# Output projection of a decoder block: half of its inner dimension as seven products of halves instead of eight, with some low parts made by GpSimd

## The chip, the cores and the metric

One core of one Trainium2 chip. The metric is the device time of one execution in microseconds (us); the kernel before takes 858.08 us, the median of three runs.

## The reference, cut to what matters

The kernel computes a hybrid decoder block in float32 on 512 tokens of width 1024: a stick-breaking attention branch and an RWKV-7 branch, merged by sigmoid gates, an output projection, a squared-ReLU MLP, per-layer embeddings and a final norm. The change lies between the merge and the MLP:

```
m = sb_up * sigmoid(gate_sb) + (rw @ w_up_rw) * sigmoid(gate_rw)   # 512 x 1024, the merged tiles
x = x + m @ w_out                                                   # 1024 x 1024, the output projection
h = rms_norm(x, mlp_norm_g)                                         # input of the MLP's first product
```

## The kernel before, in words

**Products.** TensorE multiplies float32 as three products of a reduced format (fp32r): every operand is held as a high part, which ScalarE makes by a cast, and a low part, the source minus the high part, which VectorE makes by a subtraction (`split`, L266; for weights `fetch_to`, L221 and L222). Each product of a 128 x 128 block with a 128 x 512 block is then three matmuls into one PSUM tile: high by high, high by low, low by high (`mm3`, lines L237 to L239, weights stationary; `rows3`, lines L252 to L254, activations stationary and weights moving).

**Weights.** They come in units of 128 x 1024 (512 KB), in the fixed list `seq`. SyncE loads each into one of four `w_raw` buffers; `fetch_to` then casts and subtracts up to three units ahead of the one in use (`AHEAD`), as the matmuls count down in `step`. A unit named in `homes` gets buffers of its own (`wo..`), which stay until the last token tile.

**The merge.** For m = 0 to 7 (the loop at L1128) 12 matmuls multiply the RWKV branch `orw` by half a unit of `w_up_rw` into one PSUM tile; the gate `gb` (loaded by SyncE at L1132) gets a sigmoid on ScalarE (L1134); VectorE multiplies it with the PSUM tile (L1142) and adds the other branch `ga` (loaded at L1131, added at L1143); and `split` writes the high and low parts of the merged tile into `mg0` and `mg1`, 128 channels by 512 tokens each. After the last sigmoid ScalarE loads the table of logarithm and exponential (L1137). The four tiles of the residual `xs` (512 KB each) and `praw` (512 KB) are loaded ahead of the loop (L1123, L1125).

**The output projection.** A unit of `w_out` holds 256 of the 1024 inner channels for one half of the 1024 columns: units 0 to 3 are the first half of the columns, 4 to 7 the second. `by_token` (L1077) makes the first half of the columns, 4 units x 4 token tiles x 6 matmuls, into four PSUM tiles; then, for each token tile in turn, 4 units x 6 matmuls make the second half. That is 192 matmuls of 128 x 512. `taken` (L1151) adds a finished PSUM tile to `xs` and sums its squares, `scaled` (L1162) makes the row scale and writes `xsc`, and `gained` (L1083) transposes `xsc` on TensorE (L1093) and splits it into `hx0` and `hx1`, the input of the MLP (ScalarE at L1097, VectorE at L1098).

**Order.** Each engine and each DMA queue does its instructions in the order in which the program lists them; a framework works this order out from the code's order, the buffers and the dependences. GpSimd does nothing in this stretch before.

Of the kernel before, what the change touches and what calls it, by code (L numbers as in the profile page):

```python
# [10 lines left out]
F32 = mybir.dt.float32  # L11
# [7 lines left out]
P = 128  # L19
# [72 lines left out]
def tile_block(ctx: ExitStack, tc: tile.TileContext, xT, xt, pT, wts, lora, cols_d, gfin_d, consts_d, out, dbg=None):  # L92
# [5 lines left out]
    def r32(ap):  # L98
        return ap.bitcast(F32)
# [106 lines left out]
    def fetch_to(n, ahead=0):  # L206
        while state["i"] < min(n, len(seq)):
            i = state["i"]
            state["i"] += 1
            load_to(i + 1 + ahead)  # L210
            raw = made(i)
            if seq[i] in homes:
                hi, lo = homes[seq[i]]()
            elif seq[i][0] == U_S4:
                hi = wpool.tile([P, 512], F32R, name="w_hi4", bufs=1)
                lo = wpool.tile([P, 512], F32R, name="w_lo4", bufs=1)
            else:
                hi = wpool.tile([P, 1024], F32R, name="w_hi")
                lo = wpool.tile([P, 1024], F32R, name="w_lo")
            with tc.issue_after(state["hx"]) if seq[i] == (U_FF1, 4) else nullcontext():  # L220
                state["cast"] = act.copy(out=hi, in_=raw).ins  # L221
            state["wlo"] = dve.tensor_tensor(out=lo, in0=raw, in1=r32(hi), op=ALU.subtract).ins  # L222
            ready.setdefault(seq[i], []).append((hi, lo))

    def weights(*u):
# [21 lines left out]
    def rows3(ps, w, rhs, tt, k, first, last, cs=slice(0, 512)):  # L247

        xh, xl = (r[:, :, tt * P:(tt + 1) * P] for r in rhs)
        for j in range(2):  # L250
            wh, wl = (p_.rearrange("p (j f) -> p j f", j=2)[:, j, cs] for p_ in w)
            pe.matmul(ps, xh[:, k + j], wh, start=first and j == 0, stop=False, skip_group_check=True)  # L252
            pe.matmul(ps, xh[:, k + j], wl, start=False, stop=False, skip_group_check=True)  # L253
            pe.matmul(ps, xl[:, k + j], wh, start=False, stop=last and j == 1, skip_group_check=True)  # L254
            step()

    def product(ps, w, rhs, nk=KT, base=0, t=slice(0, T)):
# [5 lines left out]
            mm3(ps, w, 0, rhs, k, k == 0, k == KT - 1)  # L263
            yield

    def split(hi, lo, src):  # L266
        act.copy(out=hi, in_=src)
        state["lo"] = dve.tensor_tensor(out=lo, in0=src, in1=r32(hi), op=ALU.subtract).ins

    def sum_squares(pool_, src, k, ssum):  # L270

# [51 lines left out]
    with ExitStack() as sA:  # L323
# [43 lines left out]
        with ExitStack() as s1:  # L367
# [709 lines left out]
    def by_token(u, i, rhs, half):  # L1077
# [5 lines left out]
                rows3(pss[tt], w, rhs, tt, kk * 2, kk == 0, kk == 3)  # L1083
        return pss

    def gained(gname, half, src):

        for kp in range(KT // 2):
            ps = ps_main().rearrange("p (j t) -> p j t", j=2)
            for j in range(2):  # L1090
                for t in range(2):
                    k = kp * 2 + j
                    pe.transpose(out=ps[:, j, t * P:(t + 1) * P], in_=src[:, half * 2 + t, k * P:(k + 1) * P], identity=ident)  # L1093
# [25 lines left out]
    with ExitStack() as s3:  # L1119
        p3 = s3.enter_context(tc.tile_pool(name="p3", bufs=1))  # L1120
        mg = [pa.tile([P, KT, T], F32R, name="mg0", tag="h_lo"), p3.tile([P, KT, T], F32R, name="mg1")]
        for tt in range(TT):
            sync.dma_start(out=xs[:, tt, :], in_=xt[:, tt, :])  # L1123
        praw = p3.tile([P, 2, T], F32, name="praw")
        sync.dma_start(out=praw, in_=pT)  # L1125
        for m in range(8):

            early = {0: ("mix", "mix"), 1: ("mix", "mix"), 2: ("gg", "gg")}.get(m)  # L1128
            ga, gb = (pa.tile([P, T], F32, name=n, tag=early[j], bufs=4 if early[j] == "mix" else 2) if early else
                      p3.tile([P, T], F32, name=n, bufs=3) for j, n in enumerate(("ga", "gb")))  # L1130
            sync.dma_start(out=ga, in_=upsb[:, m, :])  # L1131
            sync.dma_start(out=gb, in_=gates[:, KT + m, :])  # L1132
            with tc.issue_after(state["norm"].ins):
                last = act.activation(out=gb, in_=gb, func=AF.Sigmoid)  # L1134
            if m == 7:
                with tc.issue_after(last.ins):
                    state["load"] = act.preload_act_table_set(LNEXP)  # L1137
            if m % 2 == 0:
                w = weights(U_UPRW, m // 2)
            ps = ps_main()  # L1140
            product(ps, w, orw, nk=4, base=m % 2 * 512)
            dve.tensor_tensor(out=gb, in0=ps, in1=gb, op=ALU.mult)  # L1142
            dve.tensor_tensor(out=ga, in0=ga, in1=gb, op=ALU.add)  # L1143
# [18 lines left out]
        def scaled(tt):  # L1162
# [8 lines left out]
        pss = by_token(U_OUT, 0, mg, 0)  # L1171
        for tt in range(TT):
            taken(pss[tt], tt, 0)
        ws = [weights(U_OUT, 4 + kk) for kk in range(4)]

        for tt in range(TT):
# [424 lines left out]
```

## Time and profile before

| what | value |
|---|---|
| times of the three runs | 859.78, 858.08, 857.35 us |
| median | 858.08 us |
| the profiled execution's own time | 858.42 us |
| its span in the trace | 856.7 us |
| granted TensorE clock, mean | 0.998 |
| busy share PE / DVE / ACT / POOL | 98% / 82% / 59% / 12% |
| the merge on TensorE | 404.3 to 425.9 us |
| the output projection on TensorE | 425.9 to 471.2 us |

Times inside the trace are us from the start of the span. PE is TensorE's matmuls, DVE is VectorE, ACT is ScalarE, POOL is GpSimd, SP is SyncE; L12 is line 12 of the kernel the row belongs to. A row's `out<-in` names the tiles; the numbers behind x are counts. Matmuls overlap each other, so the duration of one record is longer than its share of the engine.

### The profile page before, as it was taken

How to read it: one execution, taken by the hardware profiler on the slowest of the kernel's cores; microseconds unless marked ns; L12 is line 12 of the kernel's file. 1: busy time of each engine (PE TensorE's matmuls, PEld its weight loads, DVE VectorE, ACT ScalarE, POOL GpSimd, SP SyncE). 2: the span in 40 equal slices, each digit the busy share in tenths (PEclk: the TensorE clock that was granted, in tenths of full speed). 3: DMA queues.
4: the chain of work that ended last, by engine and by line, in shares of the span. 5: the costliest groups of instructions: out<-in, count | busy, mean ns of one | idle time of the engine just before them, and what ended most of it. 6: DMA issues, size and time to landing. Idle time of an engine off the chain costs nothing.

```text
span 856.7 us, 14612 instructions
## 1 busy us (share of the span) xinstructions
PE 841.8 (98%) x5606; PEld 699.0 (82%) x5606; DVE 702.6 (82%) x1247; ACT 506.8 (59%) x793; POOL 102.3 (12%) x170
## 2 busy tenths in 40 slices
PE   9999999999999999999999999999999999999996
PEld 6778788877777777777888888899889989988885
DVE  7989987896987978867773597899889988997767
ACT  7888887744436253534464675468647844783843
POOL 1332431001202111020000101000110010010000
PEclk9999999999999999999999999999999999999999
DMA  8212212231120324527960676973885489275402
GB/s 322 100 50 64 85 62 86 75 99 51 63 88 26 107 79 136 162 82 244 326 220 25 204 214 162 230 199 107 229 234 146 141 243 245 88 222 144 174 23 99
DMA packets 39333, 121.08 MB, mean 141 GB/s; under 512 B 4448, under 2 KB 4448, under 8 KB 39264
## 3 DMA queue, kind: packets, MB, share of 16 engines
q1 hardware_dynamic: 34656, 103.37, 35.5%
q0 software_dynamic: 4608, 16.78, 10.7%
q8 instruction: 44, 0.72, 0.4%
q14 instruction: 25, 0.20, 0.1%
HBM read 105.46 MB, written 10.49 MB: 135 GB/s over the span
## 4 chain that ended last, share of the span: by engine, by line
PE 87%; DVE 8%; DMA 1%; issue 1%; ACT 1%; SPq 0%; DVEq 0%; ACTq 0%
PE ps_m L237 14%; PE ps_m L238 14%; PE ps_m L239 14%; PE ps_m L252 10%; PE ps_m L253 10%; PE ps_m L254 10%; PE ps_g L863 1%; PE ps_o L543 1%; PE ps_z L551 1%; PE ps_s L991 1%; PE ps_c L982 1%; PE ps_g L953 1%; DVE LX L885 1%; DVE w_lo L222 1%; DVE own L874 1%
## 5 line engine op out<-in xcount | busy, mean ns | idle before, releaser
L221 ACT CAST w_hi<-w_raw 128x1024 fp32r<-128x1024 f32 x123 | 129.1, 1051 | 121.5 <-PE ps_m L238 71.3
L222 DVE TENSOR_TENSOR w_lo<-w_raw,w_hi 128x1024 fp32r<-128x1024 f32 x123 | 150.5, 1225 | 29.9 <-ACT w_hi L221 29.3
L237 PE MATMUL ps_m<-h_hi,w_hi 128*128 128x512 f32 x320 | 130.5, 409 | 0.1
L239 PE MATMUL ps_m<-h_hi,w_lo 128*128 128x512 f32 x320 | 128.5, 402 | 0.0
L238 PE MATMUL ps_m<-h_lo,w_hi 128*128 128x512 f32 x320 | 128.3, 401 | 0.1
L239 PEld LDWEIGHTS ps_m<-h_hi,w_lo 128*128 128x128 f32 x320 | 60.4, 189 | 11.9
L237 PEld LDWEIGHTS ps_m<-h_hi,w_hi 128*128 128x128 f32 x320 | 60.8, 190 | 10.9 <-DVE gg L724 0.4
L238 PEld LDWEIGHTS ps_m<-h_lo,w_hi 128*128 128x128 f32 x320 | 60.5, 189 | 11.2 <-DVE h_lo L400 1.3
L238 PE MATMUL ps_m<-hx,w_hi 128*128 128x256 f32 (+1 forms) x208 | 65.8, 316 | 0.0
L237 PE MATMUL ps_m<-hx,w_hi 128*128 128x256 f32 (+1 forms) x208 | 65.8, 316 | 0.0
L239 PE MATMUL ps_m<-hx,w_lo 128*128 128x256 f32 (+1 forms) x208 | 65.7, 316 | 0.0
L237 PE MATMUL ps_m<-tb,w_hi 128*128 128x256 f32 x192 | 54.3, 283 | 0.0
L238 PE MATMUL ps_m<-tb,w_hi 128*128 128x256 f32 x192 | 54.3, 283 | 0.0
L239 PE MATMUL ps_m<-tb,w_lo 128*128 128x256 f32 x192 | 54.3, 283 | 0.0
L252 PE MATMUL ps_m<-w_hi,fS 128*128 128x512 f32 x128 | 49.8, 389 | 0.0
L253 PE MATMUL ps_m<-w_lo,fS 128*128 128x512 f32 x128 | 49.8, 389 | 0.0
L254 PE MATMUL ps_m<-w_hi,fS 128*128 128x512 f32 x128 | 49.8, 389 | 0.0
L238 PEld LDWEIGHTS ps_m<-hx,w_hi 128*128 128x128 f32 x208 | 39.7, 191 | 2.9 <-DVE hx L1098 0.4
L237 PEld LDWEIGHTS ps_m<-hx,w_hi 128*128 128x128 f32 x208 | 39.7, 191 | 2.8 <-ACT hx L1097 0.2
L239 PEld LDWEIGHTS ps_m<-hx,w_lo 128*128 128x128 f32 x208 | 39.7, 191 | 2.5
L252 PE MATMUL ps_m<-w_hi,fA 128*128 128x512 f32 x96 | 37.4, 389 | 0.0
L253 PE MATMUL ps_m<-w_lo,fA 128*128 128x512 f32 x96 | 37.4, 389 | 0.0
(410 smaller groups left out, 2128.6 us busy)
## 6 DMA issues: line engine op xcount, KB each, us to landing
w_raw<-in_wts_dram SPq DMA_DIRECT2D x130, 512.0 KB, 3.7
gates<-gg SPq DMA_DIRECT2D x16, 256.0 KB, 2.0
w_raw<-in_wts_dram POOLq DMA_DIRECT2D x8, 512.0 KB, 6.7
x_in<-in_xT_dram SPq DMA_DIRECT2D x8, 256.0 KB, 5.9
tmp<-gates SPq DMA_DIRECT2D x8, 256.0 KB, 3.3
upsb<-tmp SPq DMA_DIRECT2D x8, 256.0 KB, 5.0
ga<-upsb SPq DMA_DIRECT2D x8, 256.0 KB, 5.5
gb<-gates SPq DMA_DIRECT2D x8, 256.0 KB, 5.0
```

What stands on the lines that cost most here:

```text
L221: state["cast"] = act.copy(out=hi, in_=raw).ins
L222: state["wlo"] = dve.tensor_tensor(out=lo, in0=raw, in1=r32(hi), op=ALU.subtract).ins
L237: pe.matmul(ps, wh, xh[:, k, t], start=first, stop=False, skip_group_check=skip)
L238: pe.matmul(ps, wh, xl[:, k, t], start=False, stop=False, skip_group_check=skip)
L239: pe.matmul(ps, wl, xh[:, k, t], start=False, stop=last, skip_group_check=skip)
L252: pe.matmul(ps, xh[:, k + j], wh, start=first and j == 0, stop=False, skip_group_check=True)
L253: pe.matmul(ps, xh[:, k + j], wl, start=False, stop=False, skip_group_check=True)
L254: pe.matmul(ps, xl[:, k + j], wh, start=False, stop=last and j == 1, skip_group_check=True)
L543: pe.matmul(ps_o[:, j * P:T], vv[:, j, hh, :, :].rearrange("p a d -> p (a d)"), part[:, ZB[j]:ZB[j] + ZN[j]], start=j == 2 and part is wh, ...
L551: pe.matmul(zt[b][:, :n], tri, part[:, s:s + n], start=False, stop=False, skip_group_check=True)
L863: last = pe.matmul(ps[rows, k], left[rows, k, :], rhs[rows, k], start=True, stop=True)
L874: dve.tensor_tensor(out=own8[rows], in0=own, in1=b8[rows].broadcast_to([32, 8, 32]), op=ALU.mult)
```

## The change

The first half of the inner channels (merged tiles 0 to 3, units 0, 1, 4 and 5 of `w_out`) is multiplied as a 2 x 2 product of halves with seven products and a shared set of sums (the Strassen-Winograd form) instead of eight. The halves are 256 inner channels each way, 256 tokens each way and 512 columns each way. One product of halves is 12 matmuls (`run` in `by_halves`), so the seven are 84 where eight were 96; the second half of the inner channels (units 2, 3, 6 and 7) keeps its 96, now added on top of the PSUM tiles that the seven products have left. What is new besides:

- **Sums of merged tiles** (`left_sums`): eight 128 x 256 operations on VectorE, with casts and low parts of two 128 x 1024 tiles, put into the buffers `hx0` and `hx1`.
- **Sums of weights**: T3, T2 and T1 are 128 x 1024 tiles, loaded by SyncE and added to by DMAs that GpSimd issues with accumulation; T2 is added to once more after product 2. T3 and T2 are loaded between the attention and the RWKV branch, T1 at the beginning of the merge. As operands they are called s3, s2, s4 and s6 in `seq`, and each is cast and subtracted like a unit.
- **Work between the products**: `seeded`, two copies from PSUM to PSUM on ScalarE after product 0 (product 2 goes on adding to the tiles V that were copied); `aside`, four copies from PSUM to SBUF on ScalarE; and four subtractions on VectorE with PSUM operands (`rest` and W).
- **Order on TensorE**: merged tiles 0 to 5, product 0, merged tiles 6 and 7, products 2, 1, 3, 4, 5, 6, then per token tile 12 matmuls for either half of the columns. `taken` now runs for both halves in that last loop.
- **GpSimd**: the low parts of the merged tiles 4 to 7 (128 x 512) and of units 2 and 3 (128 x 1024) go from VectorE to GpSimd.
- The loads of `xs` and `praw` are issued later, `gb` and `ga` take other buffers, tiles 0 and 1 are split for their first 256 tokens only, and the scratch of the squares has one buffer in place of two.

The diff, cut to its core:

```diff
+ORDER = (0, 2, 1, 3, 4, 5, 6)
+FROM = {0: 0, 1: 1, 5: 5}
...
-    seq += [(U_UPRW, m) for m in range(4)]
-    seq += [(U_OUT, m) for m in range(8)]
+    seq += [(U_UPRW, m) for m in range(3)] + [(U_OUT, "s", ORDER[0]), (U_UPRW, 3)]
+    seq += [(U_OUT, "s", i) for i in ORDER[1:]] + [(U_OUT, m) for m in (2, 3, 6, 7)]
...
-            state["wlo"] = dve.tensor_tensor(out=lo, in0=raw, in1=r32(hi), op=ALU.subtract).ins
+            if seq[i] in ((U_OUT, 2), (U_OUT, 3)):
+                pool.tensor_tensor(out=lo, in0=raw, in1=r32(hi), op=ALU.subtract)
+            else:
+                state["wlo"] = dve.tensor_tensor(out=lo, in0=raw, in1=r32(hi), op=ALU.subtract).ins
...
+        for t, i in ((T3, 5), (T2, 0)):
+            sync.dma_start(out=t, in_=wts[UBASE[U_OUT] + i])
+        for t, more_ in ((T3, wts[UBASE[U_OUT] + 4]), (T2, T3)):
+            pool.dma_start(out=t, in_=more_, accum_op=ALU.add)
...
+        run(0, V, True)
+        between()
+        for t2 in range(2):
+            act.copy(out=seeded[t2], in_=V[t2])
+        run(2, V, False)
+        pool.dma_start(out=T2, in_=wts[UBASE[u] + 1], accum_op=ALU.add)
+        second = aside(V)
+        run(1, seeded, False)
+        run(3, W, True)
+        run(4, V, False)
+        third = aside(W)
+        for t2 in range(2):
+            dve.tensor_tensor(out=rest[t2], in0=third[t2], in1=V[t2], op=ALU.subtract)
+        run(5, W, False)
+        for t2 in range(2):
+            dve.tensor_tensor(out=W[t2], in0=W[t2], in1=second[t2], op=ALU.subtract)
+        run(6, V, False)
+        return (seeded + V, W + rest)
...
+        sync.dma_start(out=T1, in_=wts[UBASE[U_OUT]])
+        pool.dma_start(out=T1, in_=wts[UBASE[U_OUT] + 4], accum_op=ALU.add)
...
+            n = 256 if m < 2 else T
+            split(mg[0][:, m, 0:n], mg[1][:, m, 0:n], ga[:, 0:n], dve if m < 4 else pool)
+            if m in (2, 3):
+                x, y = ups[m - 2], ga
+                left_sums(S, m - 2, y[:, 0:256], y[:, 256:T], x[:, 0:256], x[:, 256:T])
...
         for tt in range(TT):
-            ps = ps_main()
-            for kk in range(4):
-                rows3(ps, ws[kk], mg, tt, kk * 2, kk == 0, kk == 3)
-            taken(ps, tt, 1)
+            for half in range(2):
+                for kk in range(2):
+                    rows3(pss[half][tt], ws[half * 2 + kk], mg, tt, 4 + kk * 2, False, kk == 1)
+                taken(pss[half][tt], tt, half)
             scaled(tt)
```

In the rows below, trailing digits of tile names are cut: T_4508 is T1. ScalarE's order before, around the table load that follows the last gate's sigmoid (`gb<-gb`):

```order
L267 CAST mg_4497<-ga 128x512
L1134 ACTIVATE gb<-gb 128x512 x3
L267 CAST mg_4497<-ga 128x512 x2
L221 CAST w_hi<-w_raw 128x1024
L221 CAST wo_4708<-w_raw 128x1024
L267 CAST mg_4497<-ga 128x512
L1134 ACTIVATE gb<-gb 128x512
L1137 ACT_TABLE_LOAD
L221 CAST wo_4710<-w_raw 128x1024
L221 CAST w_hi<-w_raw 128x1024
```

ScalarE's order after, at the same place; `COPY ps_m<-ps_m` is the second of the two `seeded` copies:

```order
L274 CAST hx_4496<-sums 128x1024
L1198 ACTIVATE gb<-gb 128x512
L225 CAST w_hi<-w_raw 128x1024
L1198 ACTIVATE gb<-gb 128x512
L1201 ACT_TABLE_LOAD
L274 CAST mg_4506<-ga 128x512
L1117 COPY ps_m<-ps_m 128x512
L225 CAST wo_4678<-w_raw 128x1024
L274 CAST mg_4506<-ga 128x512
L225 CAST w_hi<-T_4508 128x1024
```

The table load and the last two sigmoids, which stood among casts alone, now stand ahead of a copy between two of TensorE's products.

SyncE's order of DMAs before, from the last weight unit ahead of the residual on:

```order
L178 DMA w_raw<-in_wts_dram 128x1024
L1123 DMA xs<-in_xt_dram 128x1024 x4
L1125 DMA praw<-in_pT_dram 128x1024
L1131 DMA ga<-upsb 128x512
L1132 DMA gb<-gates 128x512
L1131 DMA ga<-upsb 128x512
L1132 DMA gb<-gates 128x512
L1131 DMA ga<-upsb 128x512
L1132 DMA gb<-gates 128x512
L178 DMA w_raw<-in_wts_dram 128x1024
L1132 DMA gb<-gates 128x512
L178 DMA w_raw<-in_wts_dram 128x1024
```

And after:

```order
L182 DMA w_raw<-in_wts_dram 128x1024
L1184 DMA T_4508<-in_wts_dram 128x1024
L1196 DMA gb<-gates 128x512
L1195 DMA ga<-upsb 128x512 x2
L1196 DMA gb<-gates 128x512
L1252 DMA xs<-in_xt_dram 128x1024
L1196 DMA gb<-gates 128x512
L1252 DMA xs<-in_xt_dram 128x1024 x3
L1196 DMA gb<-gates 128x512
L1253 DMA praw<-in_pT_dram 128x1024
L1196 DMA gb<-gates 128x512
L182 DMA w_raw<-in_wts_dram 128x1024
```

T1's load and those of the gates 3 to 5 (`gb`) have gone ahead of or in between the four loads of `xs`, with two loads of `ga` directly behind T1; the gates 6 and 7 stand behind the last `xs`.

VectorE's order before, from the gate of merged tile 6 on (full names; `mg1` is a merged tile's low part, `w_lo` and `wo..` those of weights):

```order
L1142 TENSOR_TENSOR gb_4656<-ps_m_4660,gb_4656 128x512
L268 TENSOR_TENSOR mg1_4498<-ga_4605,mg0_4497 128x512
L268 TENSOR_TENSOR mg1_4498<-ga_4633,mg0_4497 128x512
L1143 TENSOR_TENSOR ga_4655<-ga_4655,gb_4656 128x512
L222 TENSOR_TENSOR w_lo_4731<-w_raw_4670,w_hi_4730 128x1024
L268 TENSOR_TENSOR mg1_4498<-ga_4655,mg0_4497 128x512
L1142 TENSOR_TENSOR gb_4684<-ps_m_4689,gb_4684 128x512
L222 TENSOR_TENSOR wo01_4709<-w_raw_4758,wo00_4708 128x1024
L1143 TENSOR_TENSOR ga_4683<-ga_4683,gb_4684 128x512
L222 TENSOR_TENSOR wo11_4711<-w_raw_4788,wo10_4710 128x1024
```

VectorE's order after, from the gate of merged tile 5 on (`hx1` is the low part of the sums):

```order
L1210 TENSOR_TENSOR gb_4652<-ps_m_4656,gb_4652 128x512
L275 TENSOR_TENSOR hx1_4497<-sums_4618,hx0_4496 128x1024
L1211 TENSOR_TENSOR ga_4651<-ga_4651,gb_4652 128x512
L229 TENSOR_TENSOR w_lo_4717<-w_raw_4714,w_hi_4716 128x1024
L1210 TENSOR_TENSOR gb_4700<-ps_m_4704,gb_4700 128x512
L1211 TENSOR_TENSOR ga_4699<-ga_4699,gb_4700 128x512
L1210 TENSOR_TENSOR gb_4728<-ps_m_4733,gb_4728 128x512
L229 TENSOR_TENSOR w_lo_4769<-T1_4508,w_hi_4768 128x1024
L1211 TENSOR_TENSOR ga_4727<-ga_4727,gb_4728 128x512
L229 TENSOR_TENSOR w_lo_4792<-T3_1561,w_hi_4791 128x1024
```

The low parts of merged tiles and of two kept units have left this queue; the low parts of the sums T1 and T3 stand in it behind the last merged tiles.

More of the change, by code (lines that the diff above doesn't have):

```diff
@@ L253, in rows3 @@
             pe.matmul(ps, xh[:, k + j], wl, start=False, stop=False, skip_group_check=True)
-            pe.matmul(ps, xl[:, k + j], wh, start=False, stop=last and j == 1, skip_group_check=True)
+            state["row"] = pe.matmul(ps, xl[:, k + j], wh, start=False, stop=last and j == 1, skip_group_check=True).ins
             step()
@@ L1084, in by_token, with by_halves, run, aside @@
         return pss
+    def by_halves(u, left, V, W, seeded, rest, spare, T2, between):
+        def run(i, pss, first):
+            w = weights(u, "s", i)
+            with tc.issue_after(state["row"]) if "row" in state else nullcontext():
+                for t2 in range(2):
+                    rows3(pss[t2], w, left[i], t2, 0, first, False)
+        def aside(pss):
+            got = [spare() for _ in range(2)]
+            for t, ps in zip(got, pss):
+                act.copy(out=t, in_=ps)
+            return got
+        run(0, V, True)
[12 more added lines that the diff above has]
+        run(5, W, False)
+        for t2 in range(2):
+            dve.tensor_tensor(out=W[t2], in0=W[t2], in1=second[t2], op=ALU.subtract)
+        run(6, V, False)
+        return (seeded + V, W + rest)
+    def left_sums(S, kp, a, b, c, d):
+        sums = const.tile([P, 4, 256], F32, name="sums", tag="lora_w")
+        for out_, x, y, op in ((0, d, b, ALU.subtract), (1, c, d, ALU.subtract), (2, sums[:, 0], c, ALU.subtract), (3, a, sums[:, 2], ALU.add)):
+            dve.tensor_tensor(out=sums[:, out_], in0=x, in1=y, op=op)
+        split(S[0][:, kp * 4:kp * 4 + 4], S[1][:, kp * 4:kp * 4 + 4], sums)
+    def lefts(x, S):
+        A11, A12, A22 = ([t[:, k:k + 2, h * 256:h * 256 + 256] for t in x] for k, h in ((0, 0), (2, 0), (2, 1)))
+        S1, S3, S2, S4 = ([t[:, i::4] for t in S] for i in range(4))
+        return (A11, A12, S2, S1, S3, S4, A22)
     def gained(gname, half, src):
@@ L1121, in tile_block, with merged @@
         mg = [pa.tile([P, KT, T], F32R, name="mg0", tag="h_lo"), p3.tile([P, KT, T], F32R, name="mg1")]
[L1122 to L1130, printed above, removed]
+        S = [t[:, 0:4].rearrange("p a (b t) -> p (a b) t", b=2) for t in hx]
+        T1 = p3.tile([P, 1024], F32, name="T1")
+        sync.dma_start(out=T1, in_=wts[UBASE[U_OUT]])
+        pool.dma_start(out=T1, in_=wts[UBASE[U_OUT] + 4], accum_op=ALU.add)
+        for i, t in ((3, T1), (2, T2), (4, T3), (6, T2)):
+            sources[U_OUT, "s", i] = lambda t=t: t
+        ups, held = [], []
+        def merged(m):
+            ga = pa.tile([P, T], F32, name="ga", tag="mix", bufs=4) if m < 4 else p3.tile([P, T], F32, name="ga", bufs=2)
+            gb = pa.tile([P, T], F32, name="gb", tag="t12" if m % 3 == 2 else "gg", bufs=1 if m % 3 == 2 else 2)
+            ups.append(ga)
             sync.dma_start(out=ga, in_=upsb[:, m, :])
@@ L1170, in scaled, with last_two @@
             state["scaled"] = act.activation(out=xsc[:, tt], in_=xs[:, tt], func=AF.Copy, scale=r).ins
-        pss = by_token(U_OUT, 0, mg, 0)
-        for tt in range(TT):
-            taken(pss[tt], tt, 0)
-        ws = [weights(U_OUT, 4 + kk) for kk in range(4)]
-        for tt in range(TT):
-            ps = ps_main()
-            for kk in range(4):
-                rows3(ps, ws[kk], mg, tt, kk * 2, kk == 0, kk == 3)
-            taken(ps, tt, 1)
+        V, W, rest = [ps_main() for _ in range(2)], [], []
+        def last_two():
+            for m in (6, 7):
+                merged(m)
+            for tt in range(TT):
+                sync.dma_start(out=xs[:, tt, :], in_=xt[:, tt, :])
+            sync.dma_start(out=praw, in_=pT)
+            rest.extend(held[6:8])
+            W.extend(ps_main() for _ in range(2))
+        pss = by_halves(U_OUT, lefts(mg, S), V, W, held[4:6], rest, lambda: pa.tile([P, T], F32, name="aside", tag="mix", bufs=4),
+                        T2, last_two)
+        split(pin[0], pin[1], praw)
+        ws = [weights(U_OUT, m) for m in (2, 3, 6, 7)]
+        for tt in range(TT):
+            for half in range(2):
+                for kk in range(2):
+                    rows3(pss[half][tt], ws[half * 2 + kk], mg, tt, 4 + kk * 2, False, kk == 1)
+                taken(pss[half][tt], tt, half)
             scaled(tt)
```

27 lines of the change are left out of this document (18 added, 9 removed).

## The prediction

> **What bounds the kernel now.** I read the page's busy times first, then the chain of work that ended last.
>
> ```profile
> PE 841.8 (98%) x5606; PEld 699.0 (82%) x5606; DVE 702.6 (82%) x1247; ACT 506.8 (59%) x793; POOL 102.3 (12%) x170
> PE 87%; DVE 8%; DMA 1%; issue 1%; ACT 1%; SPq 0%; DVEq 0%; ACTq 0%
> ```
>
> TensorE is busy 98% of the span and carries 87% of the chain; VectorE is second with 82%. Then I read the stretch that the change touches, in windows: the merge, the first half of the columns, the second half. The columns are PE, PEld, DVE, ACT, POOL busy, clock, DMA share, GB/s.
>
> ```profile
> 404.20:425.90 21.70, 21.70 (x98) 17.96 (x97) 14.95 (x20) 9.77 (x13) 0.00 (x0) 1.00 0.95 321
> 425.90:445.30 19.40, 19.40 (x87) 16.09 (x86) 15.40 (x21) 11.64 (x14) 0.00 (x0) 1.00 0.75 258
> 445.30:466.70 21.40, 21.40 (x105) 17.94 (x104) 8.94 (x26) 10.50 (x27) 0.00 (x0) 1.00 0.16 50
> ```
>
> TensorE has no gap in any of them, so a matmul left out here is time won, as long as what feeds TensorE keeps up. What feeds it is fuller ahead than behind: VectorE is busy 69% and 79% of the first two windows and 42% of the third, and the DMA engines 95% of the first. The clock is granted in full and stays out of the sum.
>
> **What a matmul is worth.** The records of a 128 x 512 matmul are 0.39 us long, but the next one starts earlier: these are the first and the last starts of TensorE's rows around the output projection, and from the chain the one group of transposes between them.
>
> ```profile
> 425.87 0.39 PE L252 MATMUL ps_m<-w_hi,mg 128*128 128x512 f32 x1
> 426.10 0.39 PE L253 MATMUL ps_m<-w_lo,mg 128*128 128x512 f32 x1
> ...
> 471.17 0.39 PE L252 MATMUL ps_m<-w_hi,pins 128*128 128x512 f32 x1
> 464.12 1.75 PE ps_m L1093 x16
> 404.27 0.23 PE ps_m L237
> ```
>
> From 425.87 to 471.17 are 45.30 us; less 1.75 for the transposes, 192 matmuls took 43.55, or 0.227 each. The change takes 12 of them away: 12 x 0.227 = **2.72 us**. (Records of 0.39 would make it 4.7, which counts the overlap twice.) This is the only thing that is won, because no other engine holds TensorE up here. It is also just above 0.3% of the time, 2.57 us, which is about what a measurement of this kernel can tell from no change: if anything of the gain is lost, the result falls below that.
>
> **The change part by part.** What the other engines get, each by its nearest row:
>
> ```profile
> L222 DVE TENSOR_TENSOR w_lo<-w_raw,w_hi 128x1024 fp32r<-128x1024 f32 x9 | 11.0, 1223 | 5.4 <-ACT w_hi L221 5.4
> L1143 DVE TENSOR_TENSOR ga<-ga,gb 128x512 f32<-128x512 f32 x8 | 5.4, 689 | 0.1
> L268 DVE TENSOR_TENSOR mg<-ga,mg 128x512 fp32r<-128x512 f32 x8 | 5.4, 687 | 2.4 <-DMA upsb<-tmp 1.7 <-ACT mg L267 0.7
> L1218 DVE TENSOR_TENSOR sums<-sums,rr 128x256 f32<-128x256 f32 x16 | 6.7, 421 | 0.1
> L221 ACT CAST w_hi<-w_raw 128x1024 fp32r<-128x1024 f32 x9 | 9.4, 1047 | 5.6 <-PE ps_m L254 3.7 <-DMA w_raw<-in_wts_dram 1.4 <-PE ps_m L238 0.4
> L801 ACT COPY BKt<-ps_g 128x512 f32<-128x512 f32 x8 | 4.4, 588 | 3.0 <-PE ps_g L799 3.0
> L526 POOL TENSOR_TENSOR sums_lo<-sums,sums_hi 128x256 fp32r<-128x256 f32 x8 | 6.4, 804 | 0.7
> ```
>
> *VectorE* gains 8 sums x 0.42, two low parts of sums and three more of weights x 1.22, and four subtractions with PSUM x 0.69: 12.2 us. It loses four low parts of tiles x 0.69, two halves of such and two kept units x 1.22: 5.7. So it does 6.5 us more, nearly all of it between 404 and 445, where the windows show 10.8 us idle. *ScalarE* gains six copies x 0.59 and five casts x 1.05, 8.8 us, with 19.7 idle there. *GpSimd* gets four low parts of 512 elements a row and two of 1024. Before has none of these sizes; in proportion to the shortest record of 256, 0.74 us, they cost 1.48 and 2.96 at most, 11.8 together, and half of that if much of 0.74 is fixed. I take 11.8. They are first needed in the last loop, 404.27 + 180 x 0.227 = 445.1, and can begin at about 424, so GpSimd is done in time even with 9 us of waits. [...]
>
> None of this is TensorE's time by itself. It becomes so at two places, where TensorE's own order now waits on the chain of the merged tiles.
>
> *Place 1: product 2's second token half.* It adds to a PSUM tile that must have been copied first. That copy stands on ScalarE behind the sigmoid of gate 7 (`gb` of merged tile 7), the table load, and the cast of tile 5. TensorE gets there after 6 x 12 + 12 + 24 + 6 = 114 matmuls: 404.27 + 114 x 0.227 = 430.1. Before, gate 7 was issued at 427.24, landed 3.5 us later, and only VectorE waited on its sigmoid; the last line but two is the landing of all gates issued in the stretch:
>
> ```profile
> 427.24 0.32 SPq L1132 DMA_DIRECT2D gb<-gates  x1
> gb<-gates SPq DMA_DIRECT2D x1, 256.0 KB, 3.5
> 430.79 0.63 ACT L1134 ACTIVATE gb<-gb 128x512 f32<-128x512 f32 x1
> 431.44 1.28 ACT L1137 ACT_TABLE_LOAD   x1
> 434.65 0.61 ACT L267 CAST mg<-ga 128x512 fp32r<-128x512 f32 x1
> DMA to landing us min/median/max: 2.9/7.5/8.8
> 429.53 0.68 DVE L1143 TENSOR_TENSOR ga<-ga,gb 128x512 f32<-128x512 f32 x1
> 430.13 1.22 DVE L222 TENSOR_TENSOR w_lo<-w_raw,w_hi 128x1024 fp32r<-128x1024 f32 x1
> ```
>
> After, it may be issued once VectorE has finished tile 4. The gates of tiles 3 to 5 no longer queue behind 2.5 MB of `xs` and `praw`, so I start VectorE's row of work at 416.2, a us after tile 3's matmuls (404.27 + 48 x 0.227 = 415.2). Up to tile 4's addition it holds six steps of 0.69, four of 0.42 and two of 1.22, 8.3 us; neighbouring records overlap by 0.08 to 0.09 (429.53 and 430.13 above), so 7.2: 423.4. With the landing of 3.5 gate 7 is there at 426.9. Sigmoid 0.63, table 1.28, cast 0.61 and copy 0.59, less the overlaps, are 2.8: 429.7. That is 0.4 us ahead of TensorE. With the shortest landing, 2.9, it is 1.0 ahead; with the longest, 8.8, it is 4.9 late. I take the row of the same transfer (3.5) and charge 0.2 us, for half of a hold of VectorE by GpSimd (next) that falls in this chain.
>
> *Place 2: product 4's low weights.* The low part of T3 stands on VectorE behind tile 7's addition, whose `ga` is loaded only when GpSimd has made tile 5's low part. TensorE wants it at 404.27 + 145 x 0.227 = 437.2. From 423.4 VectorE still has to do one sum, six steps of 0.69, three low parts of weights and one of sums at 1.22, and T3's own 1.22: 10.7 us, with 12 overlaps 9.6, so 433.0. The slack is 4.2. But in the same stretch GpSimd runs, and the two hold each other up. From the attention, where GpSimd subtracts beside VectorE:
>
> ```profile
> 37.78 0.74 POOL L526 TENSOR_TENSOR sums_lo<-sums,sums_hi 128x256 fp32r<-128x256 f32 x1
> 36.76 0.67 DVE L448 TENSOR_TENSOR ql<-qT,qq 64x512 fp32r<-64x512 f32 x1
> 37.86 1.21 DVE L448 TENSOR_TENSOR ql<-qT,qq 64x512 fp32r<-64x512 f32 x1
> 50.27 0.74 POOL L526 TENSOR_TENSOR sums_lo<-sums,sums_hi 128x256 fp32r<-128x256 f32 x1
> 50.48 0.67 DVE L512 SCALAR_TENSOR_TENSOR sp<-ps_z,sp 128x512 f32<-128x512 f32 x1
> ```
>
> Beside GpSimd's 0.74 us the same VectorE operation took 1.21 in place of 0.67: 0.54 lost, 73%. The one with a PSUM operand lost nothing (0.67). Ahead of T3 GpSimd has three tiles and one unit, 3 x 1.48 + 2.96 = 7.4 us; at 73% VectorE loses up to 5.4, if each meets an operation with both operands in SBUF. That is 1.2 more than the slack; with 0.2 for ScalarE's casts in between I charge **1.4 us**. If GpSimd's work falls into VectorE's waits, it is 0; if both it and the waits add up, the 7.4 in full make 3.2.
>
> [...]
>
> *What I cost at nothing.* The page's slices of 21.4 us, and the landing of GpSimd's accumulating DMAs:
>
> ```profile
> GB/s 322 100 50 64 85 62 86 75 99 51 63 88 26 107 79 136 162 82 244 326 220 25 204 214 162 230 199 107 229 234 146 141 243 245 88 222 144 174 23 99
> w_raw<-in_wts_dram POOLq DMA_DIRECT2D x8, 512.0 KB, 6.7
> ```
>
> The loads and accumulations of T3 and T2 lie in a stretch at about 145 us where the page's slices have 86 and 75 GB/s; they add 1 MB there, and the sums are used 280 us later. T1 takes the place of the first `xs` in SyncE's queue; a DMA that accumulates took 6.7 us, GpSimd waits only to issue it, and the sum is used at 434. The bound is that the weights behind them come late, 2 us. The loads of `xs` are wanted at 447, over 20 us after they are issued. The end of the loop stays as it is: one `taken` and `scaled` behind the last matmul.
>
> *The sum.* -2.72 + 0.2 + 1.4 = -1.1 us. The profiled execution would go from 858.42 to 857.3; it stands 0.3 above the median of the three, 858.08, so the median becomes **857.0 us**.
>
> **The rivals.**
>
> *All of it is hidden.* GpSimd's work falls into VectorE's waits, gate 7 lands early: -2.72, 855.4. For it: 4.2 and 0.4 us of slack at the two places by the rows, and the idle shares of ScalarE. Against it: the slack at place 1 is thinner than the spread of one transfer.
>
> *Gate 7 comes late, and the kernel gets slower.* The DMA engines were 95% busy in the merge, and the change adds 1 MB there and just behind (T1 twice, the third addition to T2, less one plain unit), with `xs` and `praw` now ahead of gates 6 and 7. The gates' median there was 7.5 us and the longest 8.8. Place 1 decides: gate 7 must land by 427.3. At 7.5 it lands at 430.9, the copy ends at 433.7, TensorE waits 3.6; at 8.8 it waits 4.9. With place 2's 1.4 behind it that is +2.3 to +3.6: 860.4 to 861.7. Against it: the row of gate 7 itself, 3.5.
>
> *GpSimd and VectorE exclude each other in full.* Then VectorE is late by 7.4 - 4.2 = 3.2 at place 2 and 0.6 at place 1: -2.72 + 3.8 = +1.1, 859.2. For it: VectorE's 1.21; against it: the 27% that was not lost.
>
> **How the numbers follow.** Forecast 0.35 (all within 0.3%); all hidden 0.32 (its 855.4 lies 0.1 beyond the bound of 855.5, so 0.28 faster, 0.04 same); full exclusion 0.13 (0.11 same, 0.02 slower); late gate 0.20 (from 860.65 on it is slower: 0.17 slower, 0.03 same). That makes faster 0.28, same 0.53, slower 0.19. The range goes from 854.9, the hidden case less 0.5 of the 0.7 us by which the lowest of the shown runs lies under their median, to 861.5, which takes in most of the late gate.
>
> **What would show it.** Right: 84 and 96 matmuls between the merge and the MLP, 0.227 apart; a wait of TensorE of some tenths on ScalarE's copy L1117 and about a us on VectorE's low part of T3; VectorE operations of 1.8 us and more beside GpSimd's. Wrong: TensorE without a gap from 404 to 466 (all hidden), or one wait of over 3 us in product 2 with ScalarE's sigmoid behind the gate's DMA (late gate); or a new wait at 145 to 160, which I count at nothing.

## The result and the profile after

The changed kernel takes **862.76 us** (median of six runs, 860.86 to 864.06) where the kernel before takes 858.58 in the same session (857.35 to 859.78): ratio 1.0044, interval 1.0034 to 1.0055, so 3 to 5 us slower. The prediction was 857.0, with a range up to 861.5. The profiled execution took 861.19 us, 2.77 more than the 858.42 of the one before, although it has the twelve matmuls less. Busy times and the chain first:

```profile
PE 840.7 (98%) x5594; PEld 696.0 (81%) x5594; DVE 712.7 (83%) x1258; ACT 513.2 (60%) x804; POOL 118.7 (14%) x180
PE 83%; DVE 9%; issue 3%; DMA 2%; ACT 1%; POOL 1%; SPq 0%; DVEq 0%; ACTq 0%; POOLq 0%
```

TensorE has 5594 matmuls in place of 5606. Its part of the chain has gone from 87 to 83%, and GpSimd stands in the chain for the first time. Next the merge, the seven products and what follows them, in windows (columns as in the prediction):

```profile
404.00:425.00 21.00, 21.00 (x94) 17.41 (x93) 17.95 (x29) 10.33 (x15) 1.64 (x2) 1.00 0.94 314
425.00:450.00 25.00, 20.57 (x85) 15.38 (x85) 20.73 (x19) 17.72 (x23) 13.23 (x7) 1.00 0.68 206
450.00:470.00 20.00, 20.00 (x98) 16.79 (x97) 11.01 (x26) 10.30 (x26) 0.00 (x0) 1.00 0.24 80
```

The loss is all in the middle row: TensorE is idle for 4.4 of 25 us, with GpSimd busy for 13.2, and the clock is 1.00. VectorE has 19 instructions there in 20.73 us, 1.09 each. TensorE's waits from 404 to 482 (us in total, times, longest), of which the kernel before has none:

```profile
PE ps_m L260 <- DVE w_lo L229: 2.6, 3, 2.0
PE ps_m L259 <- ACT ps_m L1117: 1.7, 1, 1.7
```

The longest wait of each row stands at one of the two places that the prediction named; the two short ones, 0.3 and 0.4 us, are for the low parts of T1 (product 3) and of product 5's unit. **Place 1**, product 2's second token half, is read from SyncE's row of gate 7, the landing of `gb` in that stretch, ScalarE and TensorE:

```profile
423.55 0.33 SPq L1196 DMA_DIRECT2D gb<-gates  x1
```

```profile
DMA to landing us min/median/max: 4.8/4.8/4.8
```

```profile
428.38 0.63 ACT L1198 ACTIVATE gb<-gb 128x512 f32<-128x512 f32 x1 [0.68 <-DMA gb<-gates]
429.03 1.28 ACT L1201 ACT_TABLE_LOAD   x1
430.32 0.62 ACT L274 CAST mg<-ga 128x512 fp32r<-128x512 f32 x1
430.85 0.58 ACT L1117 COPY ps_m<-ps_m 128x512 f32<-128x512 f32 x1
```

```profile
429.35 0.39 PE L261 MATMUL ps_m<-w_hi,hx 128*128 128x512 f32 x1
431.48 0.50 PE L259 MATMUL ps_m<-w_hi,hx 128*128 128x512 f32 x1 [1.75 <-ACT ps_m L1117]
```

Gate 7 is issued at 423.55 and lands at 428.4. Sigmoid, table, cast and copy follow without a gap to 431.43, and TensorE starts 2.13 us after its last matmul instead of 0.23: 1.9 lost.

**Place 2**, product 4's low weights, is read from TensorE, VectorE and GpSimd:

```profile
439.01 0.39 PE L259 MATMUL ps_m<-w_hi,hx 128*128 128x512 f32 x1
441.37 0.50 PE L260 MATMUL ps_m<-w_lo,hx 128*128 128x512 f32 x1 [1.97 <-DVE w_lo L229]
```

```profile
432.24 0.69 DVE L1211 TENSOR_TENSOR ga<-ga,gb 128x512 f32<-128x512 f32 x1 [2.68 <-DMA ga<-upsb]
434.57 1.72 DVE L229 TENSOR_TENSOR w_lo<-T,w_hi 128x1024 fp32r<-128x1024 f32 x1 [1.04 <-ACT w_hi L225]
436.84 1.14 DVE L1211 TENSOR_TENSOR ga<-ga,gb 128x512 f32<-128x512 f32 x1 [0.55 <-DMA ga<-upsb]
437.91 3.40 DVE L229 TENSOR_TENSOR w_lo<-T,w_hi 128x1024 fp32r<-128x1024 f32 x1
```

```profile
431.03 1.28 POOL L275 TENSOR_TENSOR mg<-ga,mg 128x512 fp32r<-128x512 f32 x1 [4.06 <-ACT mg L274]
432.48 2.72 POOL L227 TENSOR_TENSOR wo<-w_raw,wo 128x1024 fp32r<-128x1024 f32 x1 [0.17 <-ACT wo L225]
435.17 2.27 POOL L275 TENSOR_TENSOR mg<-ga,mg 128x512 fp32r<-128x512 f32 x1
437.40 2.83 POOL L227 TENSOR_TENSOR wo<-w_raw,wo 128x1024 fp32r<-128x1024 f32 x1
440.18 2.28 POOL L275 TENSOR_TENSOR mg<-ga,mg 128x512 fp32r<-128x512 f32 x1
```

The last VectorE row is the low part of T3: 3.40 us for what takes 1.22 alone. It begins at 437.91, inside GpSimd's 437.40 to 440.23, and ends 1.08 us after that, at 441.31, where TensorE goes on: of the 2.32 us beside GpSimd it lost 2.18. The next GpSimd subtraction then takes 2.28 in place of 1.28, one us more, where VectorE still had 1.13 to run. So in these rows each lost nearly all that was left of the other's time, and the rows lengthen in turn.

### The profile page after: what moved, and what is told of

Same layout as the page of the kernel before. It is cut to its first block, busy times and chain, and to the rows that moved or that the text cites. A ratio compares the mean times of both kernels' runs of the same rounds, so it can differ in the third digit from the quotient of the medians.

```text
span 859.4 us, 14644 instructions
## 1 busy us (share of the span) xinstructions
PE 840.7 (98%) x5594; PEld 696.0 (81%) x5594; DVE 712.7 (83%) x1258; ACT 513.2 (60%) x804; POOL 118.7 (14%) x180
## 4 chain that ended last, share of the span: by engine, by line
PE 83%; DVE 9%; issue 3%; DMA 2%; ACT 1%; POOL 1%; SPq 0%; DVEq 0%; ACTq 0%; POOLq 0%
PE ps_m L244 14%; PE ps_m L245 14%; PE ps_m L246 13%; PE ps_m L259 9%; PE ps_m L260 9%; PE ps_m L261 9%; DVE w_lo L229 1%; PE ps_g L877 1%; PE ps_o L550 1%; PE ps_s L1005 1%; PE ps_z L558 1%; PE ps_c L996 1%; PE ps_g L967 1%; DVE LX L899 1%; DVE own L888 1%
```

## The experiments

Theory P: the low parts on GpSimd hold VectorE, and VectorE's row of work is on the path (place 2). Rivals: the late gate (place 1), VectorE's additional work whoever does it, the loads. The edits shown are of the changed kernel where nothing else is said.

**All low parts back on VectorE.**

```
-            if seq[i] in ((U_OUT, 2), (U_OUT, 3)):
-                pool.tensor_tensor(out=lo, in0=raw, in1=r32(hi), op=ALU.subtract)
-            else:
-                state["wlo"] = dve.tensor_tensor(out=lo, in0=raw, in1=r32(hi), op=ALU.subtract).ins
+            state["wlo"] = dve.tensor_tensor(out=lo, in0=raw, in1=r32(hi), op=ALU.subtract).ins
...
-            split(mg[0][:, m, 0:n], mg[1][:, m, 0:n], ga[:, 0:n], dve if m < 4 else pool)
+            split(mg[0][:, m, 0:n], mg[1][:, m, 0:n], ga[:, 0:n])
```

> The kernel after, with all low parts on VectorE again (tiles 4 to 7, units 2 and 3); seven products and everything else as after. Theory P (GpSimd and VectorE hold each other up, and that makes the low parts of T1, T3 and of unit s5 late): TensorE's waits of 0.4, 2.1 and 0.5 us on VectorE's low parts go down to a few tenths, the wait of 1.9 us in product 2 stays: 2.5 us under the kernel after, about 1.5 us over the kernel before. Theory G (gate 7 late behind the DMA traffic is what costs): nothing but the 1.9 us matters, so within 0.5 us of the kernel after. Theory V (VectorE has no room for these low parts, which is why they were moved): slower than the kernel after by 1 us or more.

Measured: 859.23 us (12 runs, 856.68 to 864.33; before 858.31), ratio 1.0012 [0.9997, 1.0026]. VectorE has 4 x 0.69 + 2 x 1.22 = 5.2 us more to do, and the kernel is some 3 us faster than the changed one. So it is not VectorE's load that makes the change slow. Its profile still has waits of 2.6 us in place of 4.3: 0.6 for the copy, 0.8 for the low weights, 1.2 for a cast. Not all of that gain is shown to be the hold's: in this profile gate 7 landed in 3.3 us, and tile 5's cast no longer stands ahead of the copy. The idle subtractions below test the hold by itself.

**The two copies ahead of tiles 6 and 7**, so that they no longer queue behind the sigmoid of gate 7:

```
         run(0, V, True)
-        between()
         for t2 in range(2):
-            act.copy(out=seeded[t2], in_=V[t2])
+            state["copied"] = act.copy(out=seeded[t2], in_=V[t2])
+        between()
```

> The kernel after, with the two copies to the seeded tiles written ahead of merged tiles 6 and 7, so that the second stands on ScalarE ahead of gate 7's sigmoid and the table load. Theory G: the 1.9 us wait in product 2 goes and comes back nowhere, 1.9 us under the kernel after. Theory P: the wait goes, but VectorE's low part of T3 is late by the same clock, so product 4 waits nearly 2 us longer (about 4 in place of 2.1): 0 to 0.6 us under the kernel after.

Measured: 861.22 (5 runs, 860.82 to 862.75), ratio 1.0032 [1.0020, 1.0044]. TensorE's waits:

```profile
PE ps_m L260 <- DVE w_lo L229: 3.1, 3, 2.2
PE ps_m L259 <- ACT w_hi L225: 1.0, 1, 1.0
```

The wait for the copy is gone (1.7), and those for the low weights and for a cast have grown by 1.5: TensorE comes earlier to tiles that are still late. The two places do not add up; the first wait had hidden part of the second. By the ratios the kernel is some 1 us faster than the changed one, more than theory P's 0.6 and less than theory G's 1.9, but the two intervals overlap.

**Both, and gate 7's sigmoid behind the second copy** (`issue_after(state["copied" if m == 7 else "norm"].ins)`):

> All low parts on VectorE, the seeded copies written ahead of merged tiles 6 and 7, and gate 7's sigmoid made to stand behind the second copy on ScalarE. Theory P: both waits go and nothing takes their place, 2.0 to 2.7 us under the kernel before. Theory G: as the copy ahead alone, about 1 us over the kernel before. If neither holds and the gain is lost elsewhere, within 1 us of the kernel after.

Measured: 858.68 (12 runs, 856.02 to 861.71), ratio 1.0001 [0.9988, 1.0014]. This misses what I expected (2.0 to 2.7 us under the kernel before). One wait was left, 2.0 us at product 3's low part of T1; on VectorE:

```profile
434.13 0.69 DVE L1208 TENSOR_TENSOR ga<-ga,gb 128x512 f32<-128x512 f32 x1 [1.52 <-DMA ga<-upsb]
434.74 0.68 DVE L1207 TENSOR_TENSOR gb<-ps_m,gb 128x512 f32<-128x512 f32 x1
435.34 1.21 DVE L226 TENSOR_TENSOR w_lo<-T,w_hi 128x1024 fp32r<-128x1024 f32 x1
```

T1's low part stands behind the addition of tile 6, which waits for its own load. And something more follows the wait: matmuls 0.43 us apart at half the clock, from 437 to 440 (clock 0.52, TensorE without a gap):

```profile
437.00:440.00 3.00, 3.00 (x9) 2.33 (x8) 2.58 (x4) 2.55 (x4) 0.00 (x0) 0.52 0.02 7
```

The same stands in the profile of e1_low_on_vector, from 438.0 to 441.0 (clock 0.62 from 437 to 440 and 0.81 from 440 to 443), behind waits of 1.2 and 0.8 us close to each other.

**GpSimd's low parts alone, in the kernel before**: those of tiles 4 to 7 and of two kept units, with the inner dimension undivided.

```
+            if seq[i] in ((U_OUT, 4), (U_OUT, 5)):
+                pool.tensor_tensor(out=lo, in0=raw, in1=r32(hi), op=ALU.subtract)
...
+            split(mg[0][:, m, :], mg[1][:, m, :], ga, dve if m < 4 else pool)
```

> The kernel before, with only the low parts of merged tiles 4 to 7 and of units 4 and 5 moved to GpSimd; eight products as before. Theory P: GpSimd and VectorE hold each other up here as well (VectorE operations of 1.7 us and more beside GpSimd's), but TensorE has no place where it waits for them at that moment, so the same as the kernel before within 0.5 us. A theory that GpSimd's low parts are slow by themselves and reach TensorE late: 1 us or more over the kernel before.

Measured: 858.25 (11 runs), ratio 0.9997 [0.9988, 1.0005], and no wait of TensorE from 404 to 482. The hold is there, 2.96 us for 1.22, in VectorE's row beside GpSimd's:

```profile
435.77 2.40 POOL L223 TENSOR_TENSOR wo<-w_raw,wo 128x1024 fp32r<-128x1024 f32 x1
436.30 2.96 DVE L225 TENSOR_TENSOR w_lo<-w_raw,w_hi 128x1024 fp32r<-128x1024 f32 x1 [1.64 <-ACT w_hi L221]
```

The same hold cost nothing here, where TensorE was not waiting for VectorE (0.9997). It is the pairing with the seven products that costs (1.0044).

**The additions of tiles 6 and 7 later, written between products 3 and 4**, on top of the edits of e3_both (all low parts on VectorE, the copies ahead, gate 7's sigmoid behind them):

```
+            if m > 5:
+                late.append((m, ga, gb))
+                return
+            summed(m, ga, gb)
...
         run(3, W, True)
+        for x in late:
+            summed(*x)
```

`summed` holds the addition, the cast and the low part that stood in `merged`.

> All low parts on VectorE, copies ahead of the last two tiles (as in e3_both), and the additions, casts and low parts of tiles 6 and 7 put behind the additions that lead up to product 4 instead of ahead of them. In e3_both TensorE's one long wait (2.0 us at 434.2) was for the low part of T1, which stood on VectorE behind tile 6's addition, itself waiting 1.52 us for its load. Theory O (order on VectorE): with that addition out of the way the wait goes, and with it the stretch at half clock behind it, so most of the 2.7 us of twelve products shows: 855.6 to 857.4 where the kernel before has 858.3, ratio 0.997 to 0.999, with no wait over 0.8 us between 425 and 460. Theory L (lateness moves on: the loads are late whatever stands ahead): tiles 6 and 7 are then missing at a later product, a wait of 1.5 to 2.5 us stands there instead, and the time is within 0.3% of before, 857.8 to 859.5.

Measured: **857.05** (11 runs, 856.02 to 860.45; before 858.26), ratio 0.9988 [0.9980, 0.9997]. By the interval that is 0.3 to 1.7 us under the kernel before. No wait is listed between 404 and 482, and the middle window is full again:

```profile
425.00:450.00 25.00, 24.91 (x107) 19.33 (x106) 24.43 (x29) 18.75 (x25) 0.87 (x1) 1.00 0.74 230
```

VectorE now does 29 instructions in 24.43 us there, 0.84 each, and is 98% busy. Theory O stands. The profiled execution took 856.49, 1.9 less than before, not 2.72. Seven matmuls between 433 and 444 start 0.33 to 0.45 us after the one ahead in place of 0.23, which makes 1.0 us in all. Each of them starts just as something that it needs is done, or is the next one behind such a start. Here it is T1's low part, which VectorE ends at 434.10:

```profile
433.78 0.39 PE L256 MATMUL ps_m<-w_hi,hx 128*128 128x512 f32 x1
434.15 0.50 PE L257 MATMUL ps_m<-w_lo,hx 128*128 128x512 f32 x1
434.49 0.39 PE L258 MATMUL ps_m<-w_hi,hx 128*128 128x512 f32 x1
```

```profile
432.88 1.22 DVE L226 TENSOR_TENSOR w_lo<-T,w_hi 128x1024 fp32r<-128x1024 f32 x1
```

T3's low part ends at 436.97 and its matmul starts at 437.03; a copy on ScalarE ends at 439.82 and a matmul starts at 439.87. So these are waits too, too short for the list: what is left of the lateness, and not a fixed price of the seven products.

**GpSimd beside VectorE, with nobody waiting.** The kernel with all low parts on VectorE, and behind the low part of each of tiles 4 to 7:

```
+                    pool.tensor_tensor(out=idle, in0=r32(mg[0][:, m, :]), in1=r32(mg[0][:, m, :]), op=ALU.subtract)
```

> The kernel of e1_low_on_vector (all low parts on VectorE, 859.2) with four further GpSimd subtractions 128x512 whose result nobody reads, one behind each of tiles 4 to 7, where the changed kernel has its four. Nothing waits for them by name. Theory P (GpSimd holds VectorE off while it works): VectorE rows that fall in GpSimd's 1.3 us are longer by the part they share, some 2 to 4 us in all between 424 and 442, and the time is 1 to 3.5 us over e1_low_on_vector, 860.2 to 862.7. Theory W (it is the wait for GpSimd's result, not its presence, that costs): nothing that is waited for has changed, 858.8 to 859.8.

Measured: 861.40 (6 runs, 859.27 to 862.49), ratio 1.0031 [1.0019, 1.0042], where e1_low_on_vector had 1.0012 [0.9997, 1.0026]. Two of its GpSimd rows and the VectorE rows beside them:

```profile
433.17 2.92 POOL L1214 TENSOR_TENSOR sqx<-mg 128x512 f32<-128x512 f32 x2 [3.69 <-ACT mg L271]
440.48 1.24 POOL L1214 TENSOR_TENSOR sqx<-mg 128x512 f32<-128x512 f32 x1 [4.39 <-ACT mg L271]
```

```profile
433.05 2.14 DVE L272 TENSOR_TENSOR mg<-ga,mg 128x512 fp32r<-128x512 f32 x2 [0.57 <-ACT mg L271]
435.12 2.06 DVE L226 TENSOR_TENSOR w_lo<-T,w_hi 128x1024 fp32r<-128x1024 f32 x1
437.09 1.21 DVE L226 TENSOR_TENSOR wo<-w_raw,wo 128x1024 fp32r<-128x1024 f32 x1
440.74 2.06 DVE L226 TENSOR_TENSOR wo<-w_raw,wo 128x1024 fp32r<-128x1024 f32 x1
```

A 1.22-us subtraction takes 2.06 in the two rows beside GpSimd's and 1.21 in the one apart from them. So here the presence of GpSimd was enough to hold VectorE; that someone waits for its result (theory W) isn't needed. TensorE's waits for low weights are 2.4 us here, against 0.8 in e1_low_on_vector. The wait for the copy grew too, from 0.6 to 1.6; gate 7 landed in 4.4 us here and in 3.3 there, so that part of the time is not shown to be GpSimd's.

**Half of it each: only the tiles', or only the units' low parts on GpSimd.** Each is the changed kernel with one of the two edits of the first experiment.

> The changed kernel with the low parts of the two weight units back on VectorE; those of the four tiles stay on GpSimd. Theory P splits the 3.5 us between the changed kernel (862.8) and e1_low_on_vector (859.2) by GpSimd's time in the stretch: four times 1.28 us here of 5.1 + 5.4 in all, so about half: 860.5 to 861.8. Theory U (only the big subtractions of the units beside product 4's low weights matter): 859.0 to 860.0.

> The changed kernel with the low parts of the four tiles back on VectorE; those of the two weight units stay on GpSimd, 2.7 us each. Theory P: about half of the 3.5 us, 860.5 to 861.8. Theory U (the units' subtractions carry it, since one of them lies beside product 4's low weights): 861.8 to 863.2. The wait in product 2 for ScalarE's copy stays in both, about 1.7 us.

Measured: 860.97 (6 runs), ratio 1.0037 [1.0024, 1.0051], with the tiles on GpSimd; 861.38 (5 runs), ratio 1.0031 [1.0019, 1.0043], with the units. Either is enough to lose most of it, and neither alone carries it. Theory U falls for the tiles (at most 860.0, where the interval begins at 860.3); for the units its 861.8 lies just inside the interval's end, 861.9. Which costs more, these intervals don't tell. The idle subtractions above cost about as much as the tiles' real ones (1.0031 and 1.0037).

**A wait by hand**, to see what the half clock is. In the kernel before, behind the first token tile of the last loop, five or seven times:

```
+            if tt == 0:
+                for _ in range(5):
+                    act.copy(out=mg[0][:, 0:2, :], in_=r32(mg[0][:, 0:2, :]))
             taken(ps, tt, 1)
```

> The kernel before, with one wait put in by hand at a place where nothing else is short: after the products of the first token tile of the second half of columns, ScalarE casts merged tiles 0 and 1 onto themselves five times, 128x1024 at 1.05 us (start to start 0.95), and the next token tile's first matmuls need them. ScalarE is free from about 449.5, TensorE wants the tiles at 451.7, so it waits 2.3 to 3 us. Theory H (a wait is followed by a stretch at half clock): matmuls after it start 0.43 us apart instead of 0.227 for up to 3.3 us in some of the runs, and the time is 2.3 to 4.6 us over before. Theory S (a wait costs its own length, and the slow matmuls in e1_low_on_vector and e3_both had another reason, such as VectorE and the loads beside them): 0.227 us throughout, 2.3 to 3.0 over before, and the runs lie as close together as those of the kernel before.

> The same with seven casts: TensorE waits 4 to 6 us. [...] Theory S: 0.227 us at once after the wait, and the time over before is the wait alone.

Measured: five casts 860.50 (10 runs, 859.80 to 861.68; before 858.53), ratio 1.0023 [1.0013, 1.0032]; seven 865.63 (4 runs, 864.21 to 865.95), ratio 1.0077 [1.0062, 1.0092]. The wait with five casts, and what follows it:

```profile
453.53 0.39 PE L254 MATMUL ps_m<-w_hi,mg 128*128 128x512 f32 x1
455.54 0.50 PE L252 MATMUL ps_m<-wo,mg 128*128 128x512 f32 x1 [1.62 <-ACT mg L1182]
455.87 0.40 PE L253 MATMUL ps_m<-wo,mg 128*128 128x512 f32 x1
```

With seven:

```profile
452.70 0.39 PE L254 MATMUL ps_m<-w_hi,mg 128*128 128x512 f32 x1
457.39 0.79 PE L252 MATMUL ps_m<-wo,mg 128*128 128x512 f32 x1 [4.31 <-ACT mg L1182]
457.99 0.63 PE L253 MATMUL ps_m<-wo,mg 128*128 128x512 f32 x1
...
462.25 0.63 PE L254 MATMUL ps_m<-wo,mg 128*128 128x512 f32 x1
462.68 0.54 PE L252 MATMUL ps_m<-wo,mg 128*128 128x512 f32 x1
463.06 0.40 PE L253 MATMUL ps_m<-wo,mg 128*128 128x512 f32 x1
```

The short wait costs its own length: 1.8 us, with 0.1 more at the next start, 1.9 of the 1.97 measured; what I expected of theory H for it, up to 4.6, did not come. But the wait came out at 1.6 us and not at the 2.3 to 3 that I had planned, so this does not try a wait of 2 us. The long one costs 4.5, and then 13 matmuls take 5.67 us, from 457.39 to 463.06, in place of 13 x 0.227 = 2.95: 2.7 more, together 7.2, where 7.1 was measured. Nothing else was short there, so the half clock follows from the wait itself, at this length.

**The loads beside gate 7.** In the changed kernel the four loads of `xs` and that of `praw` put behind the seven products; and, apart from it, T1's two loads left out, so that product 3 multiplies with T3 in place of T1:

> The changed kernel with the loads of the input rows (xs, four of 512 KB) and of praw put behind the seven products instead of beside the loads of tiles 6 and 7. Theory D (loads beside it keep gate 7 back): gate 7 lands 2.8 to 3.7 us after its issue instead of 4.8, the copy that waits behind its sigmoid comes earlier, and product 2's second half waits 0.3 to 1.0 us instead of 1.9; the time falls to 860 to 862. Theory N (the landing of a small load here does not hang on these): 4.3 to 5.3 us, wait and time as in the changed kernel, 862 to 863.5.

> The changed kernel without the two loads that make T1 (product 3 takes T3's weights; the result is not the reference's). This takes one plain and one accumulating load of 512 KB out of 407 to 424, and VectorE's and ScalarE's work stays. Theory D: with less in flight the input rows, gates 6 and 7 and tile 6 land 0.5 to 2 us earlier, product 2's wait falls to 0.3 to 1.2 us, and the time is 860 to 862. Theory N: landings as in the changed kernel within 0.5 us, and the time 862 to 863.5.

Measured: 865.00 (4 runs), ratio 1.0077 [1.0062, 1.0092], and 864.50 (4 runs), ratio 1.0067 [1.0045, 1.0090]. Gate 7 took, in this order,

```profile
DMA to landing us min/median/max: 3.5/3.5/3.5
```

```profile
DMA to landing us min/median/max: 3.2/3.2/3.2
```

This is what theory D expected, but it does not show it. With the loads of `xs`, `praw` and T1 as in the changed kernel, gate 7 took 3.3, 3.4 and 3.4 us in the profiles of e1_low_on_vector, e2_copy_ahead and e7_only_tiles_on_pool, and 4.4 to 5.0 in the changed kernel, e3_both, e5_additions_late, e6_idle_pool_beside and e8_only_units_on_pool. And in the first of the two kernels above, two of the four `xs` were still issued ahead of it, at 413.85. So what keeps the gate back stays open. On the time both theories miss. ScalarE's order has changed with the edits: the first of the two copies too stands behind gate 7's sigmoid and the table load, so TensorE waits already at product 2's first half, right behind the merge, and in the first of these kernels gate 7 is also issued only at 426.50. The waits for the copy are 5.9 and 2.1 us, each with matmuls at half clock behind it (mean granted clock 0.994 in either profile, 0.997 and 0.998 in the runs of the kernel before beside them). The edits moved more than the loads, so they don't say what the gate's lateness costs either.

## Why the prediction was wrong

- *What a matmul is worth* held: 0.227 us, and twelve fewer. In e5_additions_late, with the long waits gone, 1.9 of the 2.72 show, and the 1.0 of short waits explains what is missing (with 0.2 to spare).
- *What bounds the kernel* held: no engine but TensorE, until the change; then its order waits for the chain of merged tiles, for most of the time at the two places named. No wait is at 145 to 160, as costed.
- **The step that failed at place 1: "I take the row of the same transfer (3.5)".** The issue was right (423.4 against 423.55), in part by luck: VectorE's row of work began at 415.43 and not at 416.2, and waited 0.69 us for a cast on the way. The landing was 4.8, and with the same loads ahead of it the other profiles have anything from 3.3 to 5.0: one row was no measure for a slack of 0.4. What decides within that spread stays open. Against 0.4 us of slack stand 1.3 more of landing, 0.4 more in the issue and the chain of sigmoid to copy (its end 431.43, not 429.7), and TensorE was there at 429.6, not 430.1: 1.9 lost where 0.2 was charged. The late gate was a rival, with its condition met (it landed after 427.3), at a chance of 0.20; it had priced the wait from 3.6 on. In e5_additions_late, with the copies ahead of the sigmoid, a landing of 5.0 makes no wait there.
- **The step that failed at place 2: "433.0. The slack is 4.2".** It counted VectorE's work in one piece from 423.4 on. The low part of T3 ended at 441.31, 8.3 us later. VectorE waited for loads and a cast in the rows above (2.68, 1.04, 0.55: 4.3 us), and was held in four instructions: 3.40, 1.72 and 1.14 above in place of 1.22, 1.22 and 0.69, and 0.5 in the sums' low part at 425.51. That is 3.6 us. The hold was less than what I charged (5.4), but the waits had taken the slack of 4.2 that was to swallow it. The prediction named this case ("if both it and the waits add up") and still counted the slack in it. Of the 3.40 alone 2.2 is hold, and TensorE waited 2.0.
- *The two are one chain.* Gate 7's lateness delays the cast of tile 5, so GpSimd's low part of it (431.03), so the load of tile 7's `ga` (issued at 432.34, when GpSimd had done), so the addition at 436.84, behind which T3's low part stands. (T3's cast on ScalarE ended at 437.54, so without that addition it could have begun 0.4 us earlier and not more.) I had added the places as if they were apart; e2_copy_ahead shows that they aren't.
- *Full exclusion*, held to be less likely for "the 27% that was not lost", is what the trace shows. The attention's VectorE row began 0.08 us after GpSimd's and ended 0.55 after GpSimd's end, where it takes 0.67 alone; T3's ended 1.08 after GpSimd's end, where it takes 1.22. So each lost all that was left of GpSimd's time but 0.12 to 0.14 us, and the 27% (0.20 of 0.74) is these 0.08 and 0.12. GpSimd itself was cheaper than charged: 1.28 and 2.40 us where nothing held it, 9.9 in all in place of 11.8.
- *The sum.* TensorE's starts come late by 2.0 us at place 1, 2.2 at place 2, 0.5 at T1's low part, 0.6 at product 5's unit and 0.4 at the start of the last loop: 5.7, where 0.2 and 1.4 were charged. Less 2.72 that makes 3.0 where the profiled execution shows 2.77. The late gate and the full exclusion were rivals that each came true in kind; that both come together was not priced, and the result lies above either. The median of the runs is 1.6 us above the profiled execution. In two of the six runs (862.93 and 864.06) the granted clock is 0.995, as in the profile of e3_both with its stretch at half clock, and 0.998 in the four others, so half clock can be part of it there; two more (862.75 and 862.78) have 0.998, and for them it stays open. So does which of GpSimd's two halves costs more.

## What to carry to other kernels

Before cutting work from a saturated engine, write down for each operand when it is ready, with every wait of its producers in it, and check what of the slack is left: a slack that is worked out from busy time alone is none. Work moved from VectorE to GpSimd cost nothing where nobody waited for VectorE during that time (0.9997 in e4_pool_alone), and TensorE a wait of 2.0 us where it needed T3's low part. Beside VectorE instructions with two SBUF operands I would count GpSimd's duration as VectorE's: in the changed kernel T3's low part and the four other rows that it lengthened lost all that was left of it but 0.13 to 0.15 us, while the two with a PSUM operand (L1210, at 424.91 and 432.85) took 0.68, as that line does without GpSimd. When one wait on a chain is taken away, look for where the lateness shows next (here a queue's order did more than its load: the version that wins does all on VectorE, 98% busy, in another order).

## What the runs showed of the hardware

**A wait of TensorE cost more than its length in some of these kernels.** After a wait of 4.3 us (e10_gap_long) the matmuls start 0.43 us apart for 5 us, after 2.0 us (e3_both) and after 2.1 and 1.8 us (e12_no_t1_loads) for about 3.3 us. After 1.6 us (e9_gap_short) there is none of it, and none either after 2.0 in the changed kernel's profiled execution, 2.3 in e8_only_units_on_pool, 1.8 in e7_only_tiles_on_pool, or 1.0 and 2.2 with one matmul between them in e2_copy_ahead. So for waits of about 2 us the length alone does not decide; what does is not shown. Clock 0.50 to 0.52 in the slow windows; those of e10_gap_long, with 1.00 on both sides:

```profile
449.00:452.00 3.00, 3.00 (x15) 2.47 (x14) 1.25 (x3) 2.94 (x5) 0.00 (x0) 1.00 0.26 51
457.50:462.50 5.00, 5.00 (x12) 3.94 (x13) 0.47 (x2) 1.15 (x1) 0.00 (x0) 0.50 0.00 0
463.50:468.00 4.50, 4.50 (x21) 3.71 (x20) 1.07 (x3) 1.22 (x4) 0.00 (x0) 1.00 0.00 0
```
